# Scores of two heads on the two halves of the array's rows, and the scaled maximum taken with the bias sum

## The chip, the core and the metric

The kernel runs on one core of a Trainium2 chip. TensorE (PE in the profile; its weight loads are PEld) multiplies, VectorE (DVE), ScalarE (ACT) and GpSimd (POOL) do the rest, and the SP queue issues most transfers. The metric is the device time of one launch in microseconds, as the median of several runs.

## What is computed

A decoder trunk of two layers on 512 tokens of width 1024, in float32. Layer 0 has eight heads of attention with a forgetting bias and eight heads of sliding-window attention (window 128, two key heads, a sink per head), then a dense gated feed-forward part. Layer 1 has an indexer that scores all keys with eight small heads and keeps the best 128 per query, sixteen attention heads (four key heads) over the kept keys, then two of eight experts per token. The scores that the change is about, cut from the reference:

```python
# forgetting attention, per block of 128 queries
s = jnp.einsum('bqhd,bkhd->bhqk', qi, k, preferred_element_type=jnp.float32) * scale
s = s + ci[..., :, None] - cum[..., None, :]
s = jnp.where(kpos[None, :] <= qpos[:, None], s, -jnp.inf)
p = jax.nn.softmax(s, axis=-1)
# sliding window: the same on bands of 256 keys, with a sink in the softmax
# indexer of layer 1
logits = jnp.einsum('bqhd,bsd->bqhs', iqi, ik, preferred_element_type=jnp.float32)
score = jnp.einsum('bqh,bqhs->bqs', iwi, jax.nn.relu(logits))
_, idx = lax.top_k(score, topk)
# attention over the kept keys, four query heads per key head
s = jnp.einsum('bqhgd,bqthd->bhgqt', qi, ks, preferred_element_type=jnp.float32) * scale
```

All heads have 64 dimensions.

## The kernel before

TensorE's fast float32 format keeps only the upper part of a number, so the kernel splits each operand into a high part and a remainder (low) and sums products of parts. A projection takes three passes per 128 rows of the weights (lines 306 to 308). Activations lie transposed: the feature in the partition, the token in the free dimension. One projected block of 128 features holds two heads, the first in partitions 0 to 63 (`lo`), the second in 64 to 127 (`hi`).

For scores the contraction has only 64 rows, half of the array. `q_stack` uses the other half: for each head it builds one tile whose one half holds q's high part and whose other half holds q's low part, by two casts on ScalarE (lines 555 and 556) and two subtractions (lines 557 and 558). The second subtraction goes to GpSimd in layer 1, where the tile has more than four buffers. `k_dup` splits k per head and copies each part to the other half by a DMA (line 572). One call of `scores` then makes two passes on all 128 rows, against k's high and k's low part (lines 581 and 582), plus a pass that adds the causal or band mask where there is one (line 584, bf16):

```python
q = qs[:, j, t * P:(t + 1) * P]
T.matmul(o[:, :nk], q, kd[:, jk, 0, k0:k0 + nk], start=True, stop=False)
T.matmul(o[:, :nk], q, kd[:, jk, 1, k0:k0 + nk], start=False, stop=mask is None)
```

A call is for one head and one tile of 128 queries; 256 to 512 keys, 256 at least. There are 32 calls in the forgetting attention, 32 in the window, 24 in the indexer and 64 in the sparse attention.

`full_part` serves forgetting and sparse attention, two tiles of queries at a time. Its `front` takes a PSUM bank per head (tag "s", two buffers in all), calls `scores`, then VectorE adds the bias (or the selection) and finds the row maximum in one instruction (line 628, a custom one with an accumulator that is read by a second instruction), scales both maxima by -1/8 (line 631), ScalarE takes the exponentials and their row sums (line 633), and VectorE inverts the sums (line 635). Its `back` transposes the probabilities on TensorE (line 646), copies them out, multiplies with v on halves of the array's columns (line 657) and scales by the inverse sums (`inverse_rows`, line 592). `attend` interleaves the front of one part with the back of the part before. `band_pair` does the same for the window; there ScalarE reads the scores from PSUM itself.

In layer 1 the indexer's sums `sel` for query tiles 1 to 3 go through `choose`, 16 rounds of MAX8 and MATCH_REPLACE8 each (lines 967 and 968) on VectorE. Tile 1 is done before the sparse attention; tiles 2 and 3 run between the first halves of the eight head pairs (query tiles 0 and 1), and the second halves (tiles 2 and 3) need them.

The program is written with a framework that puts instructions on each engine's queue in an order that it decides when the kernel is built: an instruction whose buffers come free earlier may be placed ahead of one written earlier. Each engine then works through its queue in order, and a wait holds up all that stands behind it.

Whole-array work and work on a part of the array alternate on TensorE in other places too: line 657 uses halves of the columns, and the experts' overflow rows use strips of 32 columns (line 1309) and transposes on 32 rows (line 1267).

Of the kernel before, what the change touches and what calls it, by code (L numbers as in the profile page):

```python
# [19 lines left out]
P = 128  # L20
D = 1024
S = 512
# [159 lines left out]
def build(tc, I, out, dbg=None, stop=99):  # L182
# [362 lines left out]
    def q_stack(pl, src, bufs=4, bias=None):  # L545

        t = pl.tile([P, 2, S], F32R, tag="qs", name="qs", bufs=bufs)
        f = t.bitcast(F32)
        if bias is not None:
            A.activation(t[lo, 0], src[lo], AF.Identity, bias=bias[lo])  # L550
            A.activation(t[hi, 1], src[hi], AF.Identity, bias=bias[hi])
            V.scalar_tensor_tensor(t[hi, 0], src[lo], bias[lo], f[lo, 0], op0=ALU.add, op1=ALU.subtract)
            V.scalar_tensor_tensor(t[lo, 1], src[hi], bias[hi], f[hi, 1], op0=ALU.add, op1=ALU.subtract)
# [7 lines left out]
    def k_dup(pl, src, n=2, tag="kd", bufs=2, bias=None):  # L561

        t = pl.tile([P, n, 2, S], F32R, tag=tag, name="kd", bufs=bufs)
        f = t.bitcast(F32)
        for j, p in enumerate((lo, hi)[:n]):
            if bias is None:
                A.copy(t[p, j, 0], src[p])
                V.tensor_sub(t[p, j, 1], src[p], f[p, j, 0])
            else:
                A.activation(t[p, j, 0], src[p], AF.Identity, bias=bias[p])  # L570
                V.scalar_tensor_tensor(t[p, j, 1], src[p], bias[p], f[p, j, 0], op0=ALU.add, op1=ALU.subtract)
            nc.sync.dma_start(f[(hi, lo)[j], j], f[p, j])
        return t
# [38 lines left out]
    def full_part(pl, ts, qs, kd, jk, vt, hv, bias, put, mask, share):  # L612
# [50 lines left out]
    def band_pair(pl, qs, kd, jk, vt, hv, sink8, h0, put):  # L663
# [4 lines left out]
        def front():  # L668
            for t0 in (0, 2):
                for j in range(2):  # L670
                    h = h0 + j
                    s = bank("s", "s")
                    for t in (t0, t0 + 1):
# [823 lines left out]
```

## Time and profile before

| | |
|---|---|
| median of three runs | 1520.17 us (1518.06 to 1521.69) |
| profiled execution, its own time | 1520.32 us |
| its span | 1518.6 us |
| granted TensorE clock, mean share | 0.979 |
| PE / DVE / ACT / POOL busy, share of the span | 94 / 69 / 49 / 10% |

The time of an execution is 1.7 us longer than the span from its first to its last instruction. Layer 0's attention lies at 80 to 250 us, its feed-forward part ends near 670, the indexer lies at 698 to 738, sparse attention at 738 to 897, and the experts follow to the end. The ends of matmuls are modelled and overlap, so the start of the next one tells more than a duration.

### The profile page before, as it was taken

To read this page: it belongs to the slowest core of one execution; us is meant where nothing else is said; L and a number is where in the kernel's file an instruction comes from. 1 tells how busy PE (TensorE), PEld (TensorE's weight loads), DVE (VectorE), ACT (ScalarE), POOL (GpSimd) and SP (SyncE) were. 2 spreads that over 40 slices of the span, in tenths; PEclk is the share of its full clock that TensorE was granted. 3 is DMA by queue.
4 is the path that set the end of the run, shared out by engine and by line. 5 is a ranking of instruction groups with operands and counts; after the bars stand their busy time and mean duration, and the time that the engine had idled before them with its cause. 6 is when DMAs were issued, how large, how long until landed. Compare 5 with 4: busy or idle time off the path is not lost.

```text
span 1518.6 us, 23687 instructions
## 1 busy us (share of the span) xinstructions
PE 1428.2 (94%) x8595; PEld 1084.8 (71%) x8595; DVE 1048.3 (69%) x1986; ACT 745.4 (49%) x1252; POOL 150.5 (10%) x165
## 2 busy tenths in 40 slices
PE   4999999899999999989976999999999999999994
PEld 2766777677788878767855677776767777787773
DVE  5845587866674346457899853876767896887784
ACT  4544474332322222335445752755556675675672
POOL 1000000011010001003452000101010100100000
PEclk9999999999999999999998999999999999999997
DMA  8435315567574336333240103767787897898791
GB/s 313 141 120 152 105 49 180 194 208 235 179 247 142 100 125 231 88 102 105 79 126 22 43 29 105 280 222 248 245 263 257 315 340 263 281 377 242 273 376 58
DMA packets 84604, 283.23 MB, mean 187 GB/s; under 512 B 10488, under 2 KB 11272, under 8 KB 84480
## 3 DMA queue, kind: packets, MB, share of 16 engines
q1 hardware_dynamic: 70608, 233.87, 45.3%
q0 software_dynamic: 13872, 47.78, 10.6%
q8 instruction: 69, 1.13, 0.3%
q14 instruction: 55, 0.45, 0.1%
HBM read 261.28 MB, written 11.29 MB: 179 GB/s over the span
## 4 chain that ended last, share of the span: by engine, by line
PE 77%; DVE 9%; DMA 3%; issue 2%; ACT 2%; SPq 0%; POOL 0%; DVEq 0%; ACTq 0%; POOLq 0%
PE pj L306 7%; PE pj L307 7%; PE pj L308 7%; PE dn L306 4%; PE dn L308 4%; PE dn L307 4%; PE v L1309 4%; PE g L1302 3%; PE g L1304 3%; PE u L1303 3%; PE u L1302 3%; PE g L1303 3%; PE u L1304 3%; PE o L657 2%; PE yv L1309 2%
## 5 line engine op out<-in xcount | busy, mean ns | idle before, releaser
L297 ACT CAST wh<-raw 128x1024 fp32r<-128x1024 f32 (+2 forms) x404 | 399.1, 993 | 474.9 <-PE dn L307 118.4
L299 DVE TENSOR_TENSOR wl<-raw,wh 128x1024 fp32r<-128x1024 f32 (+2 forms) x394 | 449.0, 1150 | 165.9 <-ACT wh L297 160.4
L306 PE MATMUL pj<-h,wh 128*128 128x512 f32 x560 | 225.2, 404 | 3.4 <-ACT h L456 3.2
L308 PE MATMUL pj<-h,wl 128*128 128x512 f32 (+1 forms) x560 | 223.5, 400 | 0.0
L307 PE MATMUL pj<-h,wh 128*128 128x512 f32 (+1 forms) x560 | 223.1, 399 | 0.1
L376 DVE SCALAR_TENSOR_TENSOR acc<-side,sc,acc 128x512 f32<-128x512 f32 x140 | 103.5, 750 | 41.5 <-DMA side<-in_oada 36.4
L306 PEld LDWEIGHTS pj<-h,wh 128*128 128x128 f32 x560 | 106.1, 190 | 32.5 <-ACT h L456 3.7
L308 PEld LDWEIGHTS pj<-h,wl 128*128 128x128 f32 (+1 forms) x560 | 106.3, 190 | 26.1 <-issue 1.5
L307 PEld LDWEIGHTS pj<-h,wh 128*128 128x128 f32 (+1 forms) x560 | 105.8, 189 | 25.8 <-issue 1.5
L581 PE MATMUL s<-kd,qs 128*128 128x256 f32 (+2 forms) x152 | 60.0, 397 | 24.7 <-DVE st L628 17.0
L1302 PE MATMUL g<-wh,xe 128*128 128x512 f32 (+1 forms) x192 | 79.3, 413 | 1.2 <-ACT xe L1294 1.2
L1302 PE MATMUL u<-wh,xe 128*128 128x512 f32 (+1 forms) x192 | 72.8, 379 | 0.0
L1303 PE MATMUL u<-wl,xe 128*128 128x512 f32 (+1 forms) x192 | 72.7, 378 | 0.0
L1304 PE MATMUL g<-wh,xe 128*128 128x512 f32 (+1 forms) x192 | 72.4, 377 | 0.0
L1303 PE MATMUL g<-wl,xe 128*128 128x512 f32 (+1 forms) x192 | 72.2, 376 | 0.0
L1304 PE MATMUL u<-wh,xe 128*128 128x512 f32 (+1 forms) x192 | 72.2, 376 | 0.0
L308 PE MATMUL dn<-hid,wl 128*128 128x512 f32 x176 | 69.7, 396 | 0.0
L306 PE MATMUL dn<-hid,wh 128*128 128x512 f32 x176 | 69.6, 396 | 0.0
L307 PE MATMUL dn<-hid,wh 128*128 128x512 f32 x176 | 69.2, 393 | 0.0
L633 ACT ACTIVATE p<-p,st 128x128 f32<-128x128 f32 (+3 forms) x96 | 53.3, 557 | 30.2 <-DVE st L631 29.8
L1309 PE MATMUL v<-raw,xf 128*32 128x128 f32 x1760 | 67.3, 276 | 0.0
L1309 PEld LDWEIGHTS v<-raw,xf 128*32 128x32 f32 x1760 | 49.3, 109 | 21.4 <-issue 12.1
(414 smaller groups left out, 2673.3 us busy)
## 6 DMA issues: line engine op xcount, KB each, us to landing
raw<-in_xgu SPq DMA_DIRECT2D x128, 512.0 KB, 5.9
raw<-in_xdn SPq DMA_DIRECT2D x88, 512.0 KB, 4.9
side<-in_oada POOLq DMA_DIRECT2D x48, 512.0 KB, 4.2
raw<-in_xgu SPq DMA_DIRECT2D x64, 384.0 KB, 4.7
raw<-in_egu SPq DMA_DIRECT2D x44, 512.0 KB, 3.5
side<-in_eada SPq DMA_DIRECT2D x24, 512.0 KB, 6.3
raw<-in_oin SPq DMA_DIRECT2D x16, 512.0 KB, 3.6
raw<-in_ein SPq DMA_DIRECT2D x13, 512.0 KB, 4.4
```

What stands on the lines that cost most here:

```text
L297: A.copy(wh[:, :n], raw[:, :n])
L299: (G if stream["turn"] % 8 in blocks.pool else V).tensor_sub(wl[:, :n], raw[:, :n], wh[:, :n].bitcast(F32))
L306: T.matmul(out_, wh, xh, start=start, stop=False)
L307: T.matmul(out_, wh, xl, start=False, stop=False)
L308: T.matmul(out_, wl, xh, start=False, stop=stop)
L376: V.scalar_tensor_tensor(s, r, sc[:, k:k + 1], s, op0=ALU.mult, op1=ALU.add)
L581: T.matmul(o[:, :nk], q, kd[:, jk, 0, k0:k0 + nk], start=True, stop=False)
L633: A.activation(ps_[j][:, :nk], ps_[j][:, :nk], AF.Exp, bias=st[:, 1, j:j + 1], scale=SCALE, accum_out=st[:, 2, j:j + 1])
L1302: T.matmul(o, x[0], wh, start=first, stop=False)
L1303: T.matmul(o, x[0], wl, start=False, stop=False)
L1304: T.matmul(o, x[1], wh, start=False, stop=last)
L1309: T.matmul(o[32 * j:32 * j + 32], x[2], w[:, j * width:(j + 1) * width], start=first, stop=last, tile_position=(0, 32 * j), skip_group_che ...
```

## The change

`q_stack` becomes `halves`: one cast and one subtraction over all 128 partitions give a tile with the high parts of both heads and one with the low parts. In the forgetting attention k is made by the same function, without copies by DMA; the window's and layer 1's keys still come from `k_dup`, because there two query heads share one key head. `scores` now serves both heads of a pair in one call: three passes per head (high by high, high by low, low by high; low by low is left out), each on 64 rows, with the head's half of the rows given by `tile_position`, alternating between heads; the masks follow on the whole array. There are 76 calls with six half passes each, 456 in place of 304. The two banks of a pair are taken together. In `full_part` the reduction scales by -1/8 and takes the minimum, so the scaling of the maxima goes; the row sums go straight to `rc`, and one reciprocal serves both query tiles. GpSimd has no part in splitting q any more.

```diff
-    def q_stack(pl, src, bufs=4, bias=None):
-
-        t = pl.tile([P, 2, S], F32R, tag="qs", name="qs", bufs=bufs)
-        f = t.bitcast(F32)
+    def halves(pl, src, tag="qs", bufs=4, bias=None):
+
+        t = pl.tile([P, 2, S], F32R, tag=tag, name=tag, bufs=bufs)
+        f = t[:, 0].bitcast(F32)
...
-        A.copy(t[lo, 0], src[lo])
-        A.copy(t[hi, 1], src[hi])
-        V.tensor_sub(t[hi, 0], src[lo], f[lo, 0])
-        (G if bufs > 4 else V).tensor_sub(t[lo, 1], src[hi], f[hi, 1])
+        A.copy(t[:, 0], src)
+        V.tensor_sub(t[:, 1], src, f)
         return t
...
-    def scores(o, qs, j, kd, jk, t, k0, nk, mask=None, at=0):
-        q = qs[:, j, t * P:(t + 1) * P]
-        T.matmul(o[:, :nk], q, kd[:, jk, 0, k0:k0 + nk], start=True, stop=False)
-        T.matmul(o[:, :nk], q, kd[:, jk, 1, k0:k0 + nk], start=False, stop=mask is None)
-        if mask is not None:
+    def scores(os_, qs, k, t, k0, nk, mask=None, at=0):
+
+        for a, b in ((0, 0), (0, 1), (1, 0)):
+            for j, p in enumerate((lo, hi)):
+                T.matmul(os_[j][:, :nk], qs[p, a, t * P:(t + 1) * P], k[p, b, k0:k0 + nk], start=a == b,
+                         stop=a == 1 and mask is None, tile_position=(64 * j, 0))
+        for o in os_ if mask is not None else ():
             T.matmul(o[:, at:at + mask.shape[-1]], identb, mask, start=False, stop=True)
...
-                st = sm.tile([P, 3, 2], F32, name="st", tag="st", bufs=8)
-                ps_ = []
+                st = sm.tile([P, 2], F32, name="st", tag="st", bufs=8)
+                ps_ = [prob() for _ in range(2)]
+                ss = [bank("s", "s") for _ in range(2)]
+                scores(ss, qs, k, t, 0, max(nk, 256), mask, t * P)
                 for j in range(2):
-                    s = bank("s", "s")
-                    scores(s, qs, j, kd, jk[j], t, 0, max(nk, 256), mask, t * P)
-                    p = prob()
-                    V.tensor_tensor_reduce(p[:, :nk], s[:, :nk], bias(j, t)[:, :nk], scale=1.0, scalar=SEL, op0=ALU.add,
-                                           op1=ALU.max, accum_out=st[:, 0, j:j + 1])
-                    ps_.append(p)
-                V.tensor_scalar_mul(st[:, 1], st[:, 0], -SCALE)
+                    V.tensor_tensor_reduce(ps_[j][:, :nk], ss[j][:, :nk], bias(j, t)[:, :nk], scale=-SCALE, scalar=-SEL,
+                                           op0=ALU.add, op1=ALU.min, accum_out=st[:, j:j + 1])
                 for j in range(2):
-                    A.activation(ps_[j][:, :nk], ps_[j][:, :nk], AF.Exp, bias=st[:, 1, j:j + 1], scale=SCALE,
-                                 accum_out=st[:, 2, j:j + 1])
-                V.reciprocal(rc[:, i], st[:, 2])
+                    A.activation(ps_[j][:, :nk], ps_[j][:, :nk], AF.Exp, bias=st[:, j:j + 1], scale=-1.0,
+                                 accum_out=rc[:, i, j:j + 1])
                 probs.append(ps_)
                 yield
+            V.reciprocal(rc, rc)
...
             for t0 in (0, 2):
-                for j in range(2):
+                ss = [bank("s", "s") for _ in range(2)]
+                for t in (t0, t0 + 1):
+                    scores([s[:, (t - t0) * 256:] for s in ss], qs, k, t, max(t - 1, 0) * P, 256,
+                           (mband if t else mfirst).rearrange("p a b -> p (a b)"), 0)
+                for j, s in enumerate(ss):
                     h = h0 + j
...
```

Three places in the order of the instructions. The lines of the changed kernel: 575 is a half pass of the scores, 578 a mask, 621 the reduction, 628 the reciprocal, 637 the transposes, 648 the product with v, 586 the inverse sums, 554 the split of q, 957 and 958 the selection.

First, TensorE in the window attention, the second two query tiles of the first pair of heads. `s_1741` and `s_1774` are the banks of its two heads before, `s_1725` and `s_1726` after; `o` is the product with v of the part ahead. Before:

```order
L581 MATMUL s_1741<-kd_1399,qs_1490 128x256
L582 MATMUL s_1741<-kd_1399,qs_1490 128x256
L584 LDWEIGHTS identb_82
L584 MATMUL s_1741<-mband_96,identb_82 128x256
L581 MATMUL s_1741<-kd_1399,qs_1490 128x256
L582 MATMUL s_1741<-kd_1399,qs_1490 128x256
L584 LDWEIGHTS identb_82
L584 MATMUL s_1741<-mband_96,identb_82 128x256
L657 MATMUL o_1757<-pT_1702,vt_487 64x256 x5
L657 MATMUL o_1757<-pT_1702,vt_487 64x128 x2
L581 MATMUL s_1774<-kd_1399,qs_1490 128x256
L582 MATMUL s_1774<-kd_1399,qs_1490 128x256
```

and after:

```order
L575 MATMUL s_1725<-kd_1381,qs_1472 128x256 x3
L578 LDWEIGHTS identb_82
L578 MATMUL s_1725<-mband_96,identb_82 128x256
L575 MATMUL s_1725<-kd_1381,qs_1472 128x256 x3
L578 LDWEIGHTS identb_82
L578 MATMUL s_1725<-mband_96,identb_82 128x256
L648 MATMUL o_1752<-pT_1693,vt_477 64x256
L575 MATMUL s_1726<-kd_1381,qs_1472 128x256 x3
L578 LDWEIGHTS identb_82
L578 MATMUL s_1726<-mband_96,identb_82 128x256
L575 MATMUL s_1726<-kd_1381,qs_1472 128x256 x3
```

Four whole-array score passes with masks between them, and then the other head, have become four groups of three half passes of one head, each followed by a whole-array mask, with a product on column halves between the heads. The two heads do not alternate here.

Second, TensorE in the second part of the sparse attention. `s_6846` to `s_6877` before are query tiles 0 and 1 of a pair, and `s_6865` to `s_6892` after are the same; `tr` are transposes, `pr` the inverse sums. Before:

```order
L581 MATMUL s_6846<-kd_6007,qs_6656 128x256
L582 MATMUL s_6846<-kd_6007,qs_6656 128x256
L581 MATMUL s_6851<-kd_6007,qs_6656 128x256
L582 MATMUL s_6851<-kd_6007,qs_6656 128x256
L592 MATMUL pr_6789<-identf_77,rcb_6790 128x128 x2
L646 MATMUL tr_6861<-identf_77,p_6743 128x128 x3
L646 MATMUL tr_6866<-identf_77,p_6748 128x128 x3
L581 MATMUL s_6872<-kd_6007,qs_6656 128x256
L582 MATMUL s_6872<-kd_6007,qs_6656 128x256
L581 MATMUL s_6877<-kd_6007,qs_6656 128x256
L582 MATMUL s_6877<-kd_6007,qs_6656 128x256
```

and after:

```order
L586 MATMUL pr_6808<-identf_77,rcb_6809 128x128 x2
L575 MATMUL s_6865<-kd_6031,qs_6675 128x256 x3
L637 MATMUL tr_6878<-identf_77,p_6758 128x128 x3
L575 MATMUL s_6866<-kd_6031,qs_6675 128x256 x3
L637 MATMUL tr_6883<-identf_77,p_6759 128x128 x3
L575 MATMUL s_6891<-kd_6031,qs_6675 128x256 x3
L575 MATMUL s_6892<-kd_6031,qs_6675 128x256 x3
L637 MATMUL tr_6903<-identf_77,p_6780 128x128 x4
```

The two passes of each head have become three half passes in a row; the first two heads are set apart by transposes, the next two stand as three and three.

Third, VectorE in the first part of the sparse attention, around one reduction pair (`s_6412`, `s_6417` before, `s_6432`, `s_6433` after); `sel` is the selection in its rounds. Before:

```order
L968 MATCH_REPLACE sel_5421<-m8_6303,sel_5421 128x512
L631 TENSOR_SCALAR st_6389<-st_6389 128x2
L628 ISA p_6415,st_6411<-s_6412,sel_5421 128x256
L628 ISA st_6411 128x1
L967 MAX m8_6306<-sel_5421 128x8
L628 ISA p_6420,st_6411<-s_6417,sel_5421 128x256
L628 ISA st_6411 128x1
L968 MATCH_REPLACE sel_5421<-m8_6306,sel_5421 128x512
L635 RECIPROCAL rc_6388<-st_6389 128x2
L631 TENSOR_SCALAR st_6411<-st_6411 128x2
L967 MAX m8_6309<-sel_5421 128x8
L590 COPY rcb_6440<-rc_6232 128x256
```

and after:

```order
L621 ISA p_6430,st_6429<-s_6432,sel_5429 128x256
L621 ISA st_6429 128x1
L957 MAX m8_6323<-sel_5429 128x8
L554 TENSOR_TENSOR qs_6403<-rq_6393,qs_6403 128x512
L958 MATCH_REPLACE sel_5429<-m8_6323,sel_5429 128x512
L621 ISA p_6431,st_6429<-s_6433,sel_5429 128x256
L621 ISA st_6429 128x1
L957 MAX m8_6326<-sel_5429 128x8
L584 COPY rcb_6459<-rc_6251 128x256
L958 MATCH_REPLACE sel_5429<-m8_6326,sel_5429 128x512
L628 RECIPROCAL rc_6406<-rc_6406 128x4
```

The scalings of `st` are gone, two reciprocals of 128x2 have become one of 128x4, and the split of q stands there over 128 partitions.

## Rows read from the trace of the kernel before

**Rows 1.** the page, busy time by engine: us, share of the span, instructions.

```profile
PE 1428.2 (94%) x8595; PEld 1084.8 (71%) x8595; DVE 1048.3 (69%) x1986; ACT 745.4 (49%) x1252; POOL 150.5 (10%) x165
```

**Rows 2.** busy us by stretch: PE, PEld, DVE, ACT, POOL (instructions); PE clock; DMA share, GB/s.

```profile
80.00:180.00 100.00, 95.82 (x502) 65.12 (x501) 47.91 (x145) 47.32 (x110) 4.86 (x9) 0.98 0.43 131
180.00:250.00 70.00, 69.97 (x417) 50.75 (x416) 53.78 (x138) 46.86 (x134) 0.00 (x0) 1.00 0.26 82
698.00:738.00 40.00, 37.90 (x206) 31.33 (x205) 31.89 (x55) 23.31 (x44) 16.96 (x10) 0.96 0.31 80
738.00:833.00 95.00, 73.85 (x341) 54.70 (x340) 92.19 (x239) 43.04 (x99) 40.89 (x24) 0.93 0.32 89
833.00:897.00 64.00, 61.36 (x406) 44.04 (x406) 50.40 (x190) 48.57 (x151) 4.48 (x13) 0.98 0.12 34
```

**Rows 3.** TensorE's waits, 700 to 900 us: us in total, times, longest.

```profile
PE s L581 <- DVE st L628: 14.2, 8, 9.7
PE s L581 <- DVE qs L557: 7.3, 5, 4.7
```

**Rows 4.** TensorE in order of time, indexer scores: start us, us, instruction.

```profile
702.27 0.28 PE L582 MATMUL s<-kd,qs 128*128 128x256 f32 x1
702.38 0.33 PE L581 MATMUL s<-kd,qs 128*128 128x384 f32 x1
702.55 0.34 PE L582 MATMUL s<-kd,qs 128*128 128x384 f32 x1
702.73 0.40 PE L307 MATMUL pj<-h,wh 128*128 128x512 f32 x1
```

**Rows 5.** groups by line, score passes: count, busy us, mean ns, idle before.

```profile
L581 PE MATMUL s<-kd,qs 128*128 128x256 f32 (+2 forms) x152 | 60.0, 397 | 24.7 <-DVE st L628 17.0 <-DVE qs L557 7.3 <-POOL qs L558 0.3
```

**Rows 6.** TensorE in order of time, column strips of an expert's overflow.

```profile
968.75 0.40 PE L1304 MATMUL u<-wh,xe 128*128 128x512 f32 x1
969.08 1.08 PE L1309 MATMUL v<-raw,xf 128*32 128x128 f32 x32
970.09 0.50 PE L1302 MATMUL g<-wh,xe 128*128 128x512 f32 x1
970.43 0.39 PE L1303 MATMUL g<-wl,xe 128*128 128x512 f32 x1
970.66 0.40 PE L1304 MATMUL g<-wh,xe 128*128 128x512 f32 x1
```

**Rows 7.** TensorE in order of time, a 32-row transpose among whole-array work.

```profile
1103.87 0.28 PE L1267 MATMUL xeT<-identf,xg 128*128 128x128 f32 x1
1104.08 0.24 PE L1267 MATMUL xeT<-identf,xg 32*128 32x32 f32 x1
1104.25 0.50 PE L1304 MATMUL yg<-wh,hid 128*128 128x512 f32 x1
1104.59 0.44 PE L1267 MATMUL xeT<-identf,xg 128*128 128x128 f32 x2
```

**Rows 8.** TensorE in order of time, four whole transposes in attention.

```profile
792.26 0.60 PE L646 MATMUL tr<-identf,p 128*128 128x128 f32 x4
792.62 0.48 PE L307 MATMUL pj<-h,wh 128*128 128x512 f32 x1
```

**Rows 9.** VectorE, 738 to 833 us, groups by line; then line 557, min/median/max ns.

```profile
L557 DVE TENSOR_TENSOR qs<-rq,qs 64x512 fp32r<-64x512 f32 x6 | 8.7, 1446 | 0.2
L631 DVE TENSOR_SCALAR st<-st 128x2 f32<-128x2 f32 x10 | 3.3, 334 | 0.0
L635 DVE RECIPROCAL rc<-st 128x2 f32<-128x2 f32 x9 | 1.4, 155 | 0.1
L557 DVE TENSOR_TENSOR qs<-rq,qs x6: 685/1594/1767, 769.5 to 824.9; 64x512 fp32r<-64x512 f32 x6
```

**Rows 10.** GpSimd and VectorE splitting one q, in order of time.

```profile
809.64 1.29 POOL L558 TENSOR_TENSOR qs<-rq,qs 64x512 fp32r<-64x512 f32 x1 [4.16 <-ACT qs L556]
809.71 1.77 DVE L557 TENSOR_TENSOR qs<-rq,qs 64x512 fp32r<-64x512 f32 x1
```

More of the change, by code (lines that the diff above doesn't have):

```diff
@@ L565, in k_dup @@
         for j, p in enumerate((lo, hi)[:n]):
[L566 to L571, printed above, removed]
+            A.copy(t[p, j, 0], src[p])
+            V.tensor_sub(t[p, j, 1], src[p], f[p, j, 0])
             nc.sync.dma_start(f[(hi, lo)[j], j], f[p, j])
@@ L610, in flush, with full_part @@
             pass
-    def full_part(pl, ts, qs, kd, jk, vt, hv, bias, put, mask, share):
+    def full_part(pl, ts, qs, k, vt, hv, bias, put, mask, share):
         nq = len(ts) * P
@@ L661, in full_part, with band_pair @@
         attend(front(), back())
-    def band_pair(pl, qs, kd, jk, vt, hv, sink8, h0, put):
+    def band_pair(pl, qs, k, vt, hv, sink8, h0, put):
         rc = sm.tile([P, NT, 2], F32, name="rcs", tag="rcs", bufs=4)
@@ L669, in front @@
             for t0 in (0, 2):
-                for j in range(2):
+                ss = [bank("s", "s") for _ in range(2)]
[3 more added lines that the diff above has]
+                for j, s in enumerate(ss):
                     h = h0 + j
-                    s = bank("s", "s")
-                    for t in (t0, t0 + 1):
-                        scores(s[:, (t - t0) * 256:], qs, j, kd, jk, t, max(t - 1, 0) * P, 256,
-                               (mband if t else mfirst).rearrange("p a b -> p (a b)"), 0)
                     st = sm.tile([P, 4, 2], F32, name="st5", tag="st5", bufs=8)
@@ L805, in build @@
         with right("at", bufs=1) as at, prob_tiles(4):
-            kd0 = k_dup(at, first[0], bufs=3, bias=bias[:, 0:1])
-            kq = [(kd0, q_stack(at, first[1], 3, bias[:, 1:2]))]
-            kd1 = k_dup(at, first[2], bufs=3, bias=bias[:, 2:3]) if NEARLY > 2 else None
+            kq = [(halves(at, first[0], "ks", 3, bias[:, 0:1]), halves(at, first[1], "qs", 3, bias[:, 1:2]))]
+            k1 = halves(at, first[2], "ks", 3, bias[:, 2:3])
             vt = at.tile([P, NT, 8, HD], F32, name="vt")
@@ L848, in out_tile, with fox_qk, fox_pair @@
                 return lambda c, po, rr: V.tensor_mul(of[:, c], po, rr)
-            def fox_qk(kd=None):
-                kd = kd or k_dup(at, project(ein, h), bufs=3)
-                return kd, q_stack(at, project(ein, h), 3)
-            def fox_pair(m, kd, qs):
+            def fox_qk(k=None):
+                k = k or halves(at, project(ein, h), "ks", 3)
+                return k, halves(at, project(ein, h), "qs", 3)
+            def fox_pair(m, k, qs):
                 bias = []
@@ L861, in fox_pair @@
                 for half in range(2):
-                    full_part(at, (2 * half, 2 * half + 1), qs, kd, (0, 1), vt, (2 * m, 2 * m + 1), lambda j, t: bias[j], put, mdiag, True)
+                    full_part(at, (2 * half, 2 * half + 1), qs, k, vt, (2 * m, 2 * m + 1), lambda j, t: bias[j], put, mdiag, True)
             def swa_q():
-                return q_stack(at, rope(at, project(ein, h), bufs=2), 3)
+                return halves(at, rope(at, project(ein, h), bufs=2), "qs", 3)
             def swa_pair(m, qs):
-                band_pair(at, qs, kd, m // 2, vs, m // 2, sink8, 2 * m, out_tile())
+                band_pair(at, qs, kd[:, m // 2], vs, m // 2, sink8, 2 * m, out_tile())
             for m in range(3):
-                kq.append(fox_qk(None if m else kd1))
+                kq.append(fox_qk(None if m else k1))
                 fox_pair(m, *kq[m])
                 fill(later, NA)
-            kd = k_dup(at, rope(at, project(ein, h), bufs=2), bufs=3)
+            kd = k_dup(at, rope(at, project(ein, h), bufs=2), bufs=1)
             vT = t512("vT")
@@ L945, in build @@
             for m in range(4):
-                qs = q_stack(at, rope(rp, project(oin, h)), BEHIND + 2)
-                for j in range(2):
-                    hd = 2 * m + j
-                    for t in range(1, NT):
-                        nk = (t + 1) * P
-                        s = bank("s", "s")
-                        scores(s, qs, j, ikd, 0, t, 0, nk)
+                qs = halves(at, rope(rp, project(oin, h)), "qs", BEHIND + 2)
+                for t in range(1, NT):
+                    nk = (t + 1) * P
+                    ss = [bank("s", "s") for _ in range(2)]
+                    scores(ss, qs, ikd[:, 0], t, 0, nk)
+                    for j in range(2):
+                        hd = 2 * m + j
                         rl = t512("rl")
-                        A.activation(rl[:, :nk], s[:, :nk], AF.Relu)
+                        A.activation(rl[:, :nk], ss[j][:, :nk], AF.Relu)
                         if hd == 0:
@@ L1000, in dsa_q @@
             def dsa_q():
-                return q_stack(at, rope(rp, project(oin, h)), BEHIND + 2)
+                return halves(at, rope(rp, project(oin, h)), "qs", BEHIND + 2)
             def dsa_pair(half, k):
                 g = k // 2
-                full_part(at, (2 * half, 2 * half + 1), qss[k], kds[g // 2], (g % 2, g % 2), vt, (g, g), lambda j, t: sel[:, t], dsa_put(half, k), None, half == 1)
+                full_part(at, (2 * half, 2 * half + 1), qss[k], kds[g // 2][:, g % 2], vt, (g, g), lambda j, t: sel[:, t], dsa_put(half, k), None, half == 1)
             oin.pool = POOL
```

8 lines of the change are left out of this document (3 added, 5 removed).

## The prediction

> **What bounds the kernel now.** I read the page's first section, then a table of busy times by stage, then what TensorE waits for, then its instructions one by one around the scores. TensorE is busy for 94% of the span [rows 1], but the change touches only five stretches, and they have different limits [rows 2]. In layer 0's attention (80 to 250 us) TensorE is busy for 95.8 of 100 and 69.97 of 70 us: what it does longer there ends later. In the indexer (698 to 738) it is busy for 37.9 of 40. In the first part of the sparse attention (738 to 833) VectorE is busy for 92.2 of 95 us and TensorE for 73.9: VectorE is the bound there, because the top-k selection (MAX8 and MATCH_REPLACE8) shares it with the row reductions. From 833 to 897 TensorE is again busy for 61.4 of 64 us and VectorE for 50.4. What TensorE waits for in layer 1 says the same: 14.2 us for the reductions of line 628, 9.7 of them in one wait, and 7.3 us for the split of q [rows 3].
>
> Busy time flatters TensorE: a score pass of 256 columns shows 0.28 us, but the next one starts 0.11 us later, 384 columns take 0.17 to 0.18 [rows 4] and 512 columns 0.23 [rows 6]. I therefore count from start to start: 0.455 ns per column.
>
> **Part 1: the passes.** Before, 152 calls of scores issue 304 passes (152 of line 581 [rows 5] and one of line 582 for each); by shape they stream 102,400 columns, 46.6 us at 0.455 ns. After, a pair of heads has six passes on half the rows. If the two halves always ran side by side, 228 pairs with 76,800 columns would take 34.9 us; if never, 153,600 columns would take 69.9 us. The order lies between, since the scheduler has pulled the heads apart: where the bank of one head comes free first, it stands as three passes of one head, then a mask or a transpose, then three passes of the other (the first two places shown with the change). Counting neighbours of different heads over the whole order gives 121 pairs (40,704 columns) and 214 passes alone (72,192 columns), together 51.4 us: 4.8 us more than before, not 11.7 less. By stage: forgetting attention -0.5, sliding window +1.6, indexer -0.8, sparse attention first part +0.8, second part +3.7.
>
> That two row halves run side by side at all, no row shows. Four column strips do: 32 passes of 128 columns fit in 1.01 us, 0.032 each [rows 6], where 0.455 ns per column would make 0.058 of one. I take row halves to do the same, and keep the other end for the range.
>
> The Trainium skill (TensorE: Matmul & The Clock Gate, Part 3, "The mechanism") says that matmuls on different row groups run concurrently, a few ns apart. By that rule and a perfect order this part would be the gain of 11.7 us; with the order as it is, it is the 4.8 us of loss.
>
> **Part 2: switching the array.** Nearly every call now takes TensorE from whole-array work to halves and back. In the order there are 652 changes between whole array and a part of it before, and 863 after: 31 more in the forgetting attention, 53 in the window, 30 in the indexer, 30 and 60 in the two parts of the sparse attention, 7 elsewhere. Such a change is seen in the trace. A 512-column pass before column strips lasts 0.33 us to the next start where 0.23 is usual, and the first whole-array pass behind the strips 0.34 [rows 6]: 0.10 on the way in and 0.11 on the way out, as its weights are loaded with nothing beside them. The one row-strip case is nearer: a whole transpose, a transpose on 32 rows and a 512-column pass take 0.72 us from start to start (1103.87 to 1104.59, [rows 7]); by the usual distances (four whole transposes in 0.36 us [rows 8], a 512-column pass 0.23) they would take 0.41. So a round trip costs about 0.3 us, 0.15 per change. The bounds are 0 (halves change without a stop) and 0.20 (the 0.10 of the way in and the 0.11 of a bare load at both ends). I take 0.15: 4.7, 8.0, 4.5, 4.5 and 9.0 us by stage.
>
> The Trainium skill (TensorEngine Tiling (Array Packing), "Key Properties") says that a change of the tiling mode, not merely of the tile, drains TensorE. The trace agrees with its 0.10 us on the way into the strips. This rule speaks against the change: without it parts 1 and 2 would cost 4.8 us, with it some 35.
>
> Sum of both for TensorE: layer 0 +13.8 (4.2 and 9.6), indexer +3.7, sparse attention +5.3 and +12.7. Not all of it ends late, because TensorE has short gaps before scores, in which a change can hide. I let three quarters count in layer 0 (10.4) and in the second part of the sparse attention (9.5), half in the indexer (1.9), where it has 2.1 us free in 40, and nothing in the first part, where it has 21 of 95 us free.
>
> **Part 3: VectorE, ScalarE and GpSimd.** q loses one of two casts and one of two subtractions. In the stretch that VectorE bounds, its subtraction (line 557) takes 1.45 us in the mean, 6 times, 8.7 us, with a shortest of 0.685; in the one shown it takes 1.77 us while GpSimd's half of the same work (1.29 us, line 558) runs beside it [rows 9, 10]. That half goes, so I take 0.685 for the one subtraction over 128 partitions: 8.7 - 4.1 = 4.6 us. The ten scalings by -SCALE (line 631) go, 3.3 us, as the reduction makes them; the nine reciprocals become half as many, 0.7 of 1.4 us [rows 9]. VectorE thus has 8.6 us less in the stretch that it bounds. No wait is added there: the exponential of a head now needs only its own reduction. I count all 8.6; the bounds are 4.0 (GpSimd's rotary product still slows the subtraction as before) and 11 (other instructions beside line 558 get faster too). What is late next: TensorE, with 5.3 us more in 21 free ones.
>
> Elsewhere the lighter engines are not the bound: ScalarE is busy for under four fifths of every stretch [rows 2]. The copies of k by DMA, two per pair in the forgetting attention, go too, with the same queue's weight loads behind them. Both shorten the way from projection to scores; I count -1 us, bounds 0 and -3. The move of reciprocals behind both tiles costs nothing: they are read only by the next part's last step. Both banks of scores are now taken for one tile of queries, and a reduction can start only after three passes instead of two: 0.12 us later for 256 columns, with the changes of the array above. A pass that waits for the second bank holds up the projections queued behind it on TensorE; it is in the same place in the queue as the second head's pass was before, so I count nothing more for it.
>
> **The sum.** +10.4 + 1.9 + 9.5 - 8.6 - 1.0 = +12.2 us on the profiled execution's own 1520.32 us, which is 0.15 us above the median of the three runs: 1532 us.
>
> **Rivals.**
> *The halves run one after the other* (the change would not do what it says). For it: no row shows row halves together. Against: column strips do. Then passes take 69.9 instead of 51.4 us: +5.7 and +2.1 in layer 0, +5.0 in the indexer, +1.0 and +4.7 in sparse attention; with the same shares 11.8 more, 1544. Chance 0.12.
> *Every change is paid in full at 0.20 us.* For it: TensorE hardly rests in layer 0. Against: the row-strip case gives 0.15. 84 x 0.20 + 1.1 = 17.9, indexer 5.2, second part 15.7, less 9.6: +29, 1549. Chance 0.08.
> *Faster: VectorE's relief decides.* For it: the 9.7 us wait for a reduction [rows 3] ends when the selection is through, and that comes 8.6 us sooner. Against: TensorE is the bound before and after. If changes between whole array and halves cost under 0.025 us (if halves do not stop the array as strips do) or vanish in gaps, three quarters of 1.1 + 3.7 and half of -0.8 are left of the passes at no price, 3.2, against -9.6: 1514. Chance 0.15.
> *No change.* At about 0.05 us per change both sides cancel: 1520. Chance 0.10.
>
> **How the numbers follow.** The forecast has 0.55, its own range 1524 to 1545. A measurement of this kernel tells about 0.2% (3 us) from no change. Slower: 0.55 + 0.12 + 0.08 = 0.75; same 0.10; faster 0.15. The range 1513 to 1550 leaves out about half of the fastest case and half of the slowest one.
>
> **What would show it.** Passes: the two heads' score matmuls start a few ns apart where they are neighbours in the order; if they start 0.11 us apart, halves do not run together. Changes: the distance from the last whole-array pass to the first half pass is 0.1 us longer than usual, and the first pass behind the halves has 0.34 instead of 0.23. VectorE: q's subtraction at 0.69 us over 128 partitions, no 128x2 scaling, and the end of the selection 9 us nearer to the start of the layer-1 projections. Stages: layer 0's attention ends some 9 us later, the second part of the sparse attention grows from 64 to 73 us, the first shrinks from 95 to 86. I am wrong if layer 0's attention is not longer, for then the changes cost nothing.

## The result and the profile after

The changed kernel takes 1542.7 us (median of 4 runs, 1541.18 to 1545.07) beside 1520.9 of the kernel before: a ratio of 1.0145, 95% interval 1.0121 to 1.0168, so 18 to 26 us slower. (In what follows, *before* and *after* name the two kernels, and half clock means a granted TensorE clock of 1.2 instead of 2.4 GHz.) The forecast was 1532 in a range of 1513 to 1550. The profiled execution took 1542.47 us with a span of 1540.8, 22.2 more than the span before.

The page's first section stands against [rows 1]. TensorE is busy for 38 us more with 152 more passes, VectorE for 19 us less.

```profile
PE 1466.4 (95%) x8747; PEld 1094.3 (71%) x8747; DVE 1029.2 (67%) x1902; ACT 729.1 (47%) x1228; POOL 132.2 (9%) x153
```

Where the 22 us arise is read from marks that both programs have. The table gives the lengths in us between the first copy of iw (the start of the indexer), the last ReLU, the end of the selection, the last product of the sparse attention, and the end of the span, for the two kernels and for those of the experiments, which are explained below. Each row is one execution. The last column is the time up to the end of the attention that TensorE spent at half clock, added up from the clock records of the trace.

| kernel | up to the indexer | indexer | sparse, 1st part | sparse, 2nd part | behind | at half clock up to the end of the attention |
|---|---|---|---|---|---|---|
| before | 691.7 | 40.2 | 97.9 | 66.5 | 622.3 | 37.5 |
| after | 701.3 | 44.1 | 99.9 | 76.6 | 618.9 | 58.0 |
| sum_only | 693.2 | 39.4 | 94.7 | 65.6 | 615.9 | 51.2 |
| halves_only | 699.3 | 43.2 | 101.2 | 76.4 | 618.2 | 61.4 |
| whole_passes | 696.7 | 44.5 | 94.8 | 72.1 | 615.6 | 37.5 |
| dummy_half | 698.0 | 43.6 | 100.6 | 69.8 | 617.9 | 47.8 |
| dummy_whole | 696.9 | 41.2 | 99.9 | 67.3 | 620.9 | 47.8 |
| eight_mixed | 727.1 | 51.2 | 102.4 | 89.5 | 620.8 | 61.4 |
| eight_whole | 696.2 | 42.6 | 99.4 | 70.2 | 619.4 | 34.1 |
| clock_kept | 700.7 | 44.1 | 99.4 | 70.6 | 618.3 | 51.2 |
| pairs_kept | 700.1 | 44.4 | 98.1 | 79.1 | 617.7 | 54.6 |

Layer 0 costs 9.6 us, the indexer 3.9, the two parts of the sparse attention 2.0 and 10.1, and 3.4 come back behind it, where the code is the same. Up to there after is at half clock for 20.5 us more than before: 6.8 in layer 0, 9.5 and 4.2 in the two parts of the sparse attention. If TensorE were the bound all that time, half of it would be lost. So up to 10 of the 25.6 us that the change costs up to the end of the attention come with the clock; the forecast had no such term. One stage moved against the forecast: the first part of the sparse attention should have become 8.6 us shorter.

The windows of after that answer to [rows 2], cut at the new places of the same work (columns as there):

```profile
80.00:180.00 100.00, 96.92 (x510) 63.65 (x509) 42.74 (x120) 43.91 (x105) 4.86 (x9) 0.95 0.35 110
180.00:257.00 77.00, 77.00 (x450) 52.01 (x449) 51.41 (x131) 43.15 (x127) 0.00 (x0) 1.00 0.24 76
708.00:749.00 41.00, 38.45 (x216) 28.75 (x215) 32.11 (x52) 19.76 (x40) 7.11 (x5) 0.96 0.28 78
749.00:848.00 99.00, 88.58 (x374) 62.88 (x372) 85.59 (x225) 40.81 (x96) 33.82 (x19) 0.88 0.32 86
848.00:922.00 74.00, 73.17 (x445) 45.31 (x444) 47.40 (x157) 46.69 (x146) 1.93 (x11) 0.95 0.09 29
```

In the fourth row VectorE has much of the relief that was forecast: 85.6 us of work where [rows 2] has 92.2. But the stretch is not shorter, as TensorE went from 73.9 of 95 us to 88.6 of 99, at a clock of 0.88 instead of 0.93. The waits say the same. In place of the 14.2 us in [rows 3], TensorE waits 5.9 us for a reduction (700 to 920 us), and VectorE now waits for TensorE (749 to 848 us; us in total, times, longest):

```profile
PE s L575 <- DVE st L621: 5.9, 1, 5.9
PE s L575 <- ACT qs L553: 5.4, 2, 4.4
PE s L575 <- DVE qs L554: 1.6, 1, 1.6
```

```profile
DVE p L621 <- PE s L575: 6.5, 5, 2.3
DVE first L975 <- ACT rr L588: 3.2, 3, 1.5
DVE qs L554 <- ACT qs L553: 1.9, 2, 1.5
```

The passes themselves, in order of time (start us, us, instruction): first a tile of queries whose two heads stayed together, then one where they were pulled apart.

```profile
89.44 0.39 PE L307 MATMUL pj<-h,wh 128*128 128x512 f32 x1
89.67 0.40 PE L308 MATMUL pj<-h,wl 128*128 128x512 f32 x1
90.00 0.62 PE L575 MATMUL s<-ks,qs 64*128 64x256 f32 x6
90.55 0.28 PE L578 MATMUL s<-mdiag,identb 128*128 128x128 bf16 x2
90.77 1.06 PE L352 MATMUL ada<-raw,cb 128*32 128x512 f32 x8
...
861.86 0.62 PE L575 MATMUL s<-kd,qs 64*128 64x256 f32 x3
862.41 0.55 PE L637 MATMUL tr<-identf,p 128*128 128x128 f32 x3
```

The same tile of queries in the kernel before:

```profile
91.07 0.39 PE L307 MATMUL pj<-h,wh 128*128 128x512 f32 x1
91.30 0.40 PE L308 MATMUL pj<-h,wl 128*128 128x512 f32 x1
91.53 0.28 PE L581 MATMUL s<-kd,qs 128*128 128x256 f32 x1
91.65 0.28 PE L582 MATMUL s<-kd,qs 128*128 128x256 f32 x1
91.77 0.23 PE L584 MATMUL s<-mdiag,identb 128*128 128x128 bf16 x1
91.81 0.36 PE L581 MATMUL s<-kd,qs 128*128 128x256 f32 x1
92.01 0.28 PE L582 MATMUL s<-kd,qs 128*128 128x256 f32 x1
92.13 0.23 PE L584 MATMUL s<-mdiag,identb 128*128 128x128 bf16 x1
92.29 0.64 PE L352 MATMUL ada<-raw,cb 128*32 128x512 f32 x4
```

Six passes of two heads take 0.55 us from 90.00, and three passes of one head take the same 0.55 from 861.86: where both heads stand together, the halves do run side by side. In the trace the passes of the two heads start 0.003 to 0.008 us apart there. The way in costs 0.10 us: 0.33 from line 308 to the first half pass, where before has 0.23. From the first score pass to the column strips the two kernels are equal, 0.77 us (90.00 to 90.77) and 0.76 (91.53 to 92.29). So even a pair that stays together wins nothing and pays for the way in, and one pulled apart pays 0.55 twice.

### The profile page after: what moved, and what is told of

Its sections match the earlier page's. It is cut to its first block, busy times and chain, and to the rows that moved or that the text cites. A ratio compares the mean times of both kernels' runs of the same rounds, so it can differ in the third digit from the quotient of the medians.

```text
span 1540.8 us, 23874 instructions
## 1 busy us (share of the span) xinstructions
PE 1466.4 (95%) x8747; PEld 1094.3 (71%) x8747; DVE 1029.2 (67%) x1902; ACT 729.1 (47%) x1228; POOL 132.2 (9%) x153
## 3 DMA queue, kind: packets, MB, share of 16 engines
q1 hardware_dynamic: 69968, 231.78, 44.1%
## 4 chain that ended last, share of the span: by engine, by line
PE 81%; DVE 7%; DMA 3%; issue 2%; ACT 1%; DVEq 0%; SPq 0%; ACTq 0%; POOLq 0%
PE pj L306 7%; PE pj L307 7%; PE pj L308 7%; PE s L575 5%; PE dn L306 4%; PE dn L308 4%; PE dn L307 4%; PE v L1299 4%; PE g L1292 3%; PE o L648 3%; PE g L1294 3%; PE u L1293 3%; PE g L1293 3%; PE u L1292 3%; PE u L1294 3%; PE yv L1299 2%
## 5 line engine op out<-in xcount | busy, mean ns | idle before, releaser
L376 DVE SCALAR_TENSOR_TENSOR acc<-side,sc,acc 128x512 f32<-128x512 f32 x140 | 103.3, 749 | 44.6 <-DMA side<-in_oada 39.4
L575 PE MATMUL s<-kd,qs 64*128 64x256 f32 (+2 forms) x360 | 74.4, 377 | 13.1 <-DVE st L621 5.9
L575 PEld LDWEIGHTS s<-kd,qs 64*128 64x128 f32 x360 | 44.9, 200 | 41.8 <-DVE st L621 10.3
L1294 PE MATMUL u<-wh,xe 128*128 128x512 f32 (+1 forms) x192 | 72.1, 376 | 0.0
L1299 PE MATMUL v<-raw,xf 128*32 128x128 f32 x1760 | 67.3, 276 | 0.0
```

Of the source, the lines that this page charges most:

```text
L376: V.scalar_tensor_tensor(s, r, sc[:, k:k + 1], s, op0=ALU.mult, op1=ALU.add)
L575: T.matmul(os_[j][:, :nk], qs[p, a, t * P:(t + 1) * P], k[p, b, k0:k0 + nk], start=a == b, stop=a == 1 and mask is None, tile_position=(64 ...
L1294: T.matmul(o, x[1], wh, start=False, stop=last)
L1299: T.matmul(o[32 * j:32 * j + 32], x[2], w[:, j * width:(j + 1) * width], start=first, stop=last, tile_position=(0, 32 * j), skip_group_che ...
```

## The experiments

The theory: every change between whole array and halves costs TensorE time, which shows wherever TensorE is the bound. The rivals: the order (heads pulled apart, passes that run alone), the new softmax work, the clock. Ratios are against the kernel before.

**The second part of the change alone.** In the kernel before:

```diff
-V.tensor_tensor_reduce(..., scale=1.0, scalar=SEL, op0=ALU.add, op1=ALU.max, accum_out=st[:, 0, j:j + 1])
-V.tensor_scalar_mul(st[:, 1], st[:, 0], -SCALE)
+V.tensor_tensor_reduce(..., scale=-SCALE, scalar=-SEL, op0=ALU.add, op1=ALU.min, accum_out=st[:, j:j + 1])
```

> The kernel before with the second part of the change alone: the scaled minimum comes with the bias sum, one reciprocal per tile column block, scores, q and k as before. Theory (changes of the array in use cost the time): nothing is added to TensorE (its order has 656 changes against 652), 40 multiplications by the scale and 32 small reciprocals leave VectorE, which ends last in the first part of the sparse attention; 2 to 6 us faster, 1515 to 1519 beside a kernel before of 1521, most of it in that part. Rival (the new place of the softmax work in the order costs part of the 22 us): 1523 to 1530, slower. If the whole change lost its gain only because VectorE got no lighter, this run stays at 1521.

Measured: 1512.1 us, ratio 0.9935 (0.9911 to 0.9958). The direction was right and the size larger than expected: the first part of the sparse attention is 3.2 us shorter, but 6.4 of the 9.8 us of the span lie behind the attention, where no instruction differs. There TensorE's clock was at half for 17.8 us, against 29.4 before (stretches of 3.4 and 6.8 us at 958.7 and 1023.6 us are missing); half of these 11.6 us is 5.8. That an earlier arrival always spares those stretches is not shown. Up to the end of the attention it is the other way round, 51.2 us at half clock against 37.5, and over the whole execution the mean clock is the same (0.978 and 0.979). So the 10 us are not a gain of clock as a whole; in which stage they show depends on where the clock fell. In the part that VectorE bounds, before (732 to 830 us) and then this kernel (732.6 to 827.3), columns as in [rows 2]:

```profile
732.00:830.00 98.00, 78.09 (x372) 58.73 (x370) 95.02 (x244) 45.51 (x102) 43.25 (x24) 0.94 0.32 87
```

```profile
732.60:827.30 94.70, 77.11 (x373) 59.85 (x371) 91.18 (x231) 45.42 (x103) 44.93 (x25) 0.93 0.34 90
```

VectorE has 3.8 us less work and the part ends 3.3 us sooner: there its relief counts nearly in full, as long as TensorE has its 17 us free.

**The first part of the change alone.** The changed kernel with the old reduction, scaling and reciprocals put back.

```diff
-V.tensor_tensor_reduce(..., scale=-SCALE, scalar=-SEL, op0=ALU.add, op1=ALU.min, ...)
+V.tensor_tensor_reduce(..., scale=1.0, scalar=SEL, op0=ALU.add, op1=ALU.max, ...)
+V.tensor_scalar_mul(st[:, 1], st[:, 0], -SCALE)
```

> The changed kernel with the old reduction (maximum, a multiplication by the scale per tile, a reciprocal per tile): the first part of the change alone. The second part alone took 10 us off the kernel before, 3.5 of them up to the end of the attention and the rest behind it, where the half-clock stretches were 11.6 us shorter. Theory (in the changed kernel TensorE bounds both parts of the sparse attention, so the 40 multiplications and 32 reciprocals stand where VectorE waits anyway): 0 to 5 us slower than the changed kernel, 1543 to 1548. Rival (the two parts add up, each worth the same without the other): 10 us slower, 1551 to 1554.

Measured: 1542.2 us, ratio 1.0149 (1.0110 to 1.0189), the same as the whole change. So the halves alone cost 22 us, and the lighter reduction, worth 10 us without them, is worth nothing measurable beside them: the two ratios differ by 0.6 us, give or take 7. The two parts do not add up.

**Whole passes.** The changed kernel without row tiles; each score is then a sum over both heads, and the rules of the order are kept:

```diff
-T.matmul(os_[j][:, :nk], qs[p, a, t * P:(t + 1) * P], k[p, b, k0:k0 + nk], ..., tile_position=(64 * j, 0))
+T.matmul(os_[j][:, :nk], qs[:, a, t * P:(t + 1) * P], k[:, b, k0:k0 + nk], ...)
```

> The changed kernel with its three passes per head on the whole array instead of on half of its rows (so the scores are sums over both heads; all else, the number of passes, the banks, the order rules and the work of every other engine, as in the changed kernel). By the order the columns take 153,600 x 0.455 ns = 69.9 us against 51.4, +18.5, and there are 662 changes of the array against 863, -201. Theory (a change costs about 0.20 us: 0.09 of emptying and 0.11 of a weight load that nothing covers): -40 + 18.5 = -22 of TensorE, of which half to three quarters shows: 1526 to 1532 beside a changed kernel of 1543. At the price of 0.15 that was forecast: -30 + 18.5, 1534 to 1537. Rival (the heads are pulled apart and so the passes run alone, the changes cost little): +18.5 with nothing taken away, 1552 to 1557. Rival (the low clock of the first part of the sparse attention comes from passes on half of the array): the stretch at half clock there shrinks from 20 us to under 11, and of the difference some 5 us come from there alone.

Measured: 1526.9 us, ratio 1.0031 (1.0013 to 1.0049), 16 us faster than the changed kernel although its columns take 18.5 us more. That passes run alone is therefore not what costs. The time is where the theory of 0.20 us per change put it; the forecast's 0.15 gave 1534 to 1537. But the rival of the clock has its sign too: the stretch at half clock behind the wait for q is 6.8 us, not 20.5, and up to the end of the attention half clock lasts 37.5 us against 58.0, worth up to 10 of the 13.8 us gained up to there. What is left, on top of the 18.5 us of columns that whole passes add, speaks for the changes; how much of the 16 us is theirs and how much the clock's, this run does not part. The first part of the sparse attention falls from 99.9 to 94.8 us. First this kernel, then after, columns as in [rows 2]:

```profile
741.20:836.00 94.80, 81.98 (x394) 64.13 (x392) 87.96 (x227) 42.01 (x98) 33.30 (x18) 0.94 0.33 89
```

```profile
745.40:845.30 99.90, 90.90 (x395) 65.07 (x394) 86.46 (x228) 42.08 (x98) 33.45 (x18) 0.90 0.31 84
```

VectorE's work is nearly the same in both. TensorE's is 8.9 us less with whole passes, and the stage is 5.1 us shorter.

**The price of a change by itself.** One small pass ahead of every other score tile of the kernel before, on half of the rows or on all:

```diff
+if j == 0:
+    T.matmul(o[:, :64], identb[lo], mdiag[lo, :64], start=True, stop=True, tile_position=(0, 0))   # dummy_half
+    T.matmul(o[:, :64], identb, mdiag[:, :64], start=True, stop=True)                              # dummy_whole
```

> The kernel before with one more small pass (64 columns, on rows 0 to 63 of the array) ahead of the first pass of every other score tile, 76 in all, overwritten by the pass behind it. 794 changes of the array against 652 of the same kernel with that small pass on all rows (its twin in this group). Theory: 76 x (0.09 emptying + 0.11 to 0.2 of loads + 0.09 emptying + 0.11 bare load), some 25 us of TensorE against 8 of the twin; the two differ by 10 to 16 us. Rival (changes in place cost little): the two differ by less than 3 us.

> The kernel before with one more small pass (64 columns, on all 128 rows) ahead of the first pass of every other score tile, 76 in all. Theory: 76 x about 0.1 us (29 ns of columns and what of the next weight load it does not cover) = 8 us of TensorE at most, 3 to 7 us slower than the kernel before. Rival (changes cost little, passes and their loads cost): as much as its twin on half of the rows, within 3 us.

Measured: ratios 1.0087 (1.0056 to 1.0119) and 1.0030 (1.0012 to 1.0048). The two differ by 0.0057, with an uncertainty of 0.0037 from the two intervals: 9 us, give or take 6, for 142 changes. The direction is the theory's, the size (10 to 16 expected) too uncertain to use. So eight small passes were put there, alternately half and whole, against eight whole ones:

```diff
+for n in range(4 if j == 0 else 0):
+    T.matmul(o[:, :64], identb[lo], mdiag[lo, :64], ..., tile_position=(0, 0))   # eight_whole: as the next line
+    T.matmul(o[:, :64], identb, mdiag[:, :64], ...)
```

> The kernel before with eight small passes (64 columns, overwritten) ahead of the first pass of every other score tile, alternately on rows 0 to 63 and on all rows: 608 small passes, some 600 changes of the array more than its twin in this group, in the same order word for word. Theory (a change empties the array, 0.094 us as the single small passes showed in their distances, and a load of weights behind a change may stand bare): 600 x 0.094 = 56 us of TensorE more than the twin, two thirds of it on the clock: 35 to 45 us. If every change costs the forecast's 0.15: 50 to 70. Rival (changes in place cost little; the one small pass differed by 9 us with an uncertainty of 5): under 10 us.

> The twin: the same eight small passes ahead of the same score tiles, all on the whole array. Theory: 608 x (28 ns of columns, or what of a weight load they leave bare, up to 0.1) = 17 to 60 us of TensorE, of which two thirds show: 1533 to 1560; its twin 35 to 45 us above it.

Measured: 1593.3 us, ratio 1.0483 (1.0453 to 1.0513), and 1533.0, ratio 1.0100 (1.0072 to 1.0128). They differ by 0.0383, give or take 0.0041: 58 us, from 52 to 64. The traces count 763 and 164 changes of the part of the array in use up to the end of the attention; 58 over 599 is 0.10 us each. That is more than the 35 to 45 us of the theory, which let two thirds show, and inside the 50 to 70 of a price of 0.15. Up to 14 us of it may be clock, as the profiled executions have 61.4 and 34.1 us at half clock up to there. So the price is not read from the total but from the starts, at full clock. TensorE in order of time, mixed and then whole:

```profile
92.04 0.40 PE L308 MATMUL pj<-h,wl 128*128 128x512 f32 x1
92.37 0.20 PE L582 MATMUL s<-mdiag,identb 64*128 64x64 bf16 x1
92.50 0.20 PE L583 MATMUL s<-mdiag,identb 128*128 128x64 bf16 x1
92.64 0.20 PE L582 MATMUL s<-mdiag,identb 64*128 64x64 bf16 x1
92.77 0.20 PE L583 MATMUL s<-mdiag,identb 128*128 128x64 bf16 x1
```

```profile
90.46 0.40 PE L308 MATMUL pj<-h,wl 128*128 128x512 f32 x1
90.70 0.20 PE L582 MATMUL s<-mdiag,identb 128*128 128x64 bf16 x1
90.74 0.19 PE L583 MATMUL s<-mdiag,identb 128*128 128x64 bf16 x1
90.77 0.19 PE L582 MATMUL s<-mdiag,identb 128*128 128x64 bf16 x1
90.80 0.19 PE L583 MATMUL s<-mdiag,identb 128*128 128x64 bf16 x1
```

The busy time of a pass (0.19 to 0.20 us) hides it; the starts show it. They lie 0.13 us apart with a change between them and 0.03 without. The Trainium skill (TensorEngine Tiling (Array Packing), "Key Properties") says that a change of the tiling mode drains TensorE. The trace agrees, and puts 0.10 us on it.

**The low clock.** In after TensorE waits 4.4 us for q until 785 us, and its clock is at half from 784.0 to 804.5 us. Forty whole passes were put ahead of those scores:

```diff
+for _ in range(warm if i == 0 else 0):
+    T.matmul(ss[0][:, :256], identb, mband.rearrange("p a b -> p (a b)"), start=True, stop=True)
 scores(ss, qs, k, t, 0, max(nk, 256), mask, t * P)
```

> The changed kernel with 40 more passes on the whole array (256 columns of bf16 constants, some 4.5 us, into the bank that the first score pass overwrites) ahead of the first scores of the sparse attention, where TensorE waits 4.4 us for q; there its clock falls to half and stays there for 20.5 us. Theory A (the wait starts the low clock): TensorE stays busy, no fall there or one of under 7 us, 5 to 10 us less time: 1533 to 1538. Theory B (the passes on half of the array by themselves bring or hold the low clock, wait or no wait): the stretch stays at 10 us or more, 1541 to 1546. With whole-array passes behind the same wait of 4.4 us the stretch was 6.8 us long.

Measured: 1536.4 us, ratio 1.0112 (1.0072 to 1.0152). The experiment missed its aim: the scheduler put the forty passes at 769.9 us, ahead of the last projections, and the wait stayed (5.1 us), as did the 20.5 us at half clock behind it. The gain lies elsewhere, in the second part (70.6 us instead of 76.6): a half-clock stretch of 10.2 us at 845.5 is missing there, and with it the wait of 5.9 us for a reduction in which it began (0.4 us here). The time falls into the range of theory A and the stretch into that of theory B, so this run does not tell whether the wait starts the fall.

**Pairs kept together.** Each group's passes and masks chained in program order:

```diff
-for j, p in enumerate((lo, hi)):
-    T.matmul(...)
+for j, p in ((1, hi), (0, lo)):
+    with tc.issue_after(last.ins) if last else ExitStack():
+        last = T.matmul(...)
```

> The changed kernel with each score group's six half passes and its masks chained in the order of the program on TensorE's queue, the head that the order serves first in front: by the order 180 pairs that run side by side and 96 passes alone, 42.9 us of columns against 121, 214 and 51.4, but 880 changes of the array against 863. Theory (changes at 0.15 us and columns at 0.455 ns): -8.5 + 2.6 = -6 of TensorE, of which half to three quarters shows: 1538 to 1540. Rival (heads pulled apart are what costs): the whole change minus what sum_only gained hangs on it, 1525 to 1532. Rival (a pass that may not be drawn ahead leaves TensorE waiting for the second bank): 1543 to 1550, with more waits for the reduction.

Measured: 1540.0 us, ratio 1.0119 (1.0075 to 1.0163): where the theory puts it, though the interval also holds the changed kernel's 1.0145. The rival of the order, 1525 to 1532, is out: with 172 half passes that start beside another one (within 0.015 us) against 102 in after, little is won. TensorE's waits for a reduction did grow, to 9.9 us from 5.9 (745 to 850 us), as the second rival said, but the time is below its 1543.

## Why the prediction was right, and where it failed

**Right: the passes and the order.** Halves run side by side where they are neighbours, and most are not: in the trace of after 102 half passes start within 0.015 us of another, where the order gave 121 pairs, out of 456 passes. The rival of halves in series falls on the 0.55 us of six passes.

**Right: the price of a change, for another reason in part.** Forecast 0.15 us. The change alone costs 0.10 at each end, and in a group of half passes the second start comes 0.22 us after the first instead of 0.12 (the starts of one head's three passes in the group at 90.00: 90.00, 90.22, 90.34). So a way in and out costs 0.10 + 0.10 + 0.10 = 0.3 us. The trace of after has some 120 such visits to row halves up to the end of the attention, up to 36 us of TensorE. The forecast took its price from a transpose on 32 rows [rows 7] and gave its second half to a bare load; that the late second start is a load was not tried. Before has a late second start too, 0.20 us behind a mask (91.81 and 92.01), but there the first pass starts 0.04 behind the mask, so that nothing is lost; with halves both starts are late.

**Near, in part by luck: three stages.** Layer 0 up to the indexer was forecast at 10.4, or 9.4 with the 1.0 us for the lighter engines, and is 9.6 us longer. The second part of the sparse attention was forecast at 9.5 and is 10.1. The indexer was forecast at 1.9 and measures 3.9, nearly its whole 3.7 on TensorE: the half that was to hide found no cover. The forecast had no term for the clock: half of the 6.8 and 4.2 us more at half clock is up to 3.4 us of layer 0's 9.6 and 2.1 of the second part's 10.1. How close these two came is partly chance.

**Failed: part 3, the 8.6 us of VectorE in the first part of the sparse attention, counted in full, with TensorE's work there counted at nothing because "it has 21 of 95 us free".** VectorE's work did fall by 8.6 us (95.02 to 86.46). But it fell through another sum: q's one subtraction takes 1.16 us in the mean, not 0.685, 7.0 us instead of 4.1, as two of the six still run beside GpSimd's work and take 1.96 and 1.98 us, where three without it take 0.67; in its place the rotary products and sums of lines 538 and 539, 17.0 us before, take 13.1, with less of GpSimd's work in the stage (33.5 us busy, 43.3 before). The stage grew by 2.0 us because TensorE's busy time rose by 12.8 us there, not 5.3, and what was free was not free at the right moments: VectorE waits 6.5 us for half passes that it never waited for before. Part of the rise is the clock: after has 20.5 us at half clock in this stage, all of them behind the wait for q, where whole_passes has 6.8 behind the same wait; before has 11.0 in the whole stage.

```profile
L621 DVE CUSTOM_DVE_ANT_0 p<-s,sel 128x128 f32<-128x128 f32 (+3 forms) x21 | 8.2, 395 | 6.7 <-PE s L575 6.5
L554 DVE TENSOR_TENSOR qs<-rq,qs 128x512 fp32r<-128x512 f32 x6 | 7.0, 1164 | 1.9 <-ACT qs L553 1.9
```

These are VectorE's groups in after, 749 to 848 us (count, busy us, mean ns, idle before). They answer to line 557 in [rows 9]. The rotary lines, before (732 to 830 us) and after (745.4 to 845.3):

```profile
L538 DVE TENSOR_TENSOR rr<-rr,sinT 128x512 f32<-128x512 f32 x9 | 8.8, 972 | 0.0
L539 DVE TENSOR_TENSOR rq<-rq,rr 128x512 f32<-128x512 f32 x9 | 8.2, 915 | 1.0 <-POOL rq L537 1.0
```

```profile
L538 DVE TENSOR_TENSOR rr<-rr,sinT 128x512 f32<-128x512 f32 x9 | 7.0, 780 | 0.0
L539 DVE TENSOR_TENSOR rq<-rq,rr 128x512 f32<-128x512 f32 x9 | 6.1, 676 | 0.0
```

Whole passes give 5.1 us of that stage back with the same work on VectorE, and sum_only gains 3.2 there with the old scores; so it is the halves that ate the relief.

The stages show the failure plainly. Forecast were +9.4, +1.9, -8.6 and +9.5 us, and nothing behind the attention, +12.2 together; the spans have +9.6, +3.9, +2.0, +10.1 and -3.4, +22.2 together. Of the 10.0 us between them the first part of the sparse attention alone missed by 10.6; the other misses nearly cancel. The runs of the two parts of the change say the same. halves_only holds parts 1 and 2 and, of part 3, q's lighter split and the 1.0 us: 21.8 - 4.6 - 1.0 = 16.2 us by the forecast, 22 measured. The rest of part 3, 3.3 + 0.7 = 4.0 us for scalings and reciprocals, gave 10 us without the halves and nothing measurable with them. The 3.4 us that came back behind the attention have half clock for 24.9 us instead of 29.4 beside them, 2.2 us; the rest was not traced.

**Open:** what keeps the clock low for 20.5 us in after, halves_only and clock_kept. Before, sum_only and whole_passes have 6.8 us behind a wait of 4.4 to 4.7 us; pairs_kept, with more halves side by side, has 10.2 behind one of 4.9. Kernels with whole passes alone lie between 6.8 us (dummy_whole, behind a wait of 6.1) and 10.2 (eight_whole, behind one of 4.5). A second pair points the same way: behind a wait of 5.9 us for a reduction after has 10.2 us at half clock and whole_passes 6.8. That points to half passes alone on the array, but a kernel with half passes and no wait at that place was not run, and how much of the 22 us the clock makes is not shown.

## What to carry to other kernels

A change between whole-array and part-array work costs TensorE 0.10 us, and a short visit to row halves about 0.3; so count the visits in the order that the scheduler makes, not the columns saved. Do not credit one engine's relief and another's slack in the same stage: relief is worth its size only while the other engine keeps its slack. A cheap half of a change is best tried alone: here the reduction that yields the scaled negative maximum is 10 us faster than the kernel before without the halves, and worth nothing measurable with them.

## What the hardware showed beyond expectation

Whole passes of 64 columns, each with its own weight load, start 0.03 us apart (eight_whole), which is their columns at 0.455 ns, so the loads add nothing there; between modes the same passes start 0.13 apart.

A granted clock of half can last while TensorE is nearly always busy. Busy times in after behind the wait for q (784.0 to 804.5), and in its second part, which has half passes too (862 to 922); columns as in [rows 2]:

```profile
784.00:804.50 20.50, 19.36 (x58) 12.17 (x59) 13.49 (x40) 10.08 (x27) 3.73 (x3) 0.50 0.20 51
...
862.00:922.00 60.00, 59.21 (x383) 37.24 (x383) 38.00 (x131) 40.33 (x125) 1.93 (x11) 1.00 0.03 10
```

Whole passes, right behind the same wait:

```profile
779.60:786.40 6.80, 5.66 (x19) 4.99 (x20) 4.79 (x15) 4.50 (x10) 0.59 (x1) 0.50 0.29 62
786.40:800.00 13.60, 10.95 (x62) 8.47 (x60) 13.33 (x36) 7.58 (x26) 4.37 (x3) 0.88 0.29 85
```

The first is at 1.2 GHz for 20.5 us while TensorE is busy for 19.4; the second is at 2.4 GHz for 60 us with the same kind of passes, so the passes alone do not bring the clock down; with whole passes, the third, it comes back after 6.8 us. The Trainium skill (TensorE: Matmul & The Clock Gate, Part 1, "What's actually happening") says that activity releases the throttle; here busy time as the trace counts it did not, for 20.5 us.
